# Both MLP products by Strassen's scheme in a one-core encoder layer

## The chip, the cores and the metric

The kernel runs on one core of a Trainium2 chip. The metric is the device time of one execution in microseconds; the kernel before has a median of 1634.68 us over three runs (1633.24 to 1635.64). A core has five engines that work side by side, each through its own instructions in a fixed order: TensorE (PE in the profile; PEld is its weight load) multiplies matrices into eight banks of a buffer called PSUM, VectorE (DVE), ScalarE (ACT) and GpSimd (POOL) work element by element, and SyncE (SP) here issues transfers between the on-chip buffer SBUF and DRAM. An instruction that waits holds up everything behind it on its engine.

## What is computed

One encoder layer on 1024 tokens of width 1024, all in float32. The first part (norm, pooling mixer, differential attention, gates, merge) is the same in both kernels. Behind it come the output projection and the MLP, of which the change speaks:

```python
x = x + merged @ w_out[l]
h2 = rmsnorm(x, g_ffn[l])
x = x + jnp.square(jax.nn.relu(h2 @ w_up[l])) @ w_down[l]   # w_up 1024 x 4096, w_down 4096 x 1024
```

## The kernel before

*Precision.* Every large product is done three times: `split` writes a float32 tile as a high part that TensorE multiplies exactly in its fast format (a cast on ScalarE, L114) and a low part, the rest (a subtraction on VectorE, or on GpSimd for weights, L115). `mm3` then issues three matmuls, high x high (L118), high x low (L119) and low x high (L120), that add up in one PSUM bank. A full matmul has 128 x 128 weights and moves 512 columns.

*Output projection.* `out_proj(ws, t, dh)` computes 128 tokens (tile t) by 512 columns (half dh) with 24 matmuls, and VectorE adds the result to x in SBUF (L815). The order of the calls is (th, dh) = (0,0), (0,1), (1,1), (1,0), with th the half of the tokens. As soon as both halves of a token tile are there, `late_norm` brings its second norm: ScalarE squares and sums (L254), `rsq` makes the factor with a small step on VectorE and a power on GpSimd (L236, L237), VectorE multiplies two halves by factor and gain (L258), TensorE transposes eight blocks (L263) and the result is split into h2T. These transposes stand between matmuls of later output projections and of the first up products.

*MLP.* Eight chunks of 512 of the 4096 inner columns. Per chunk eight up products (128 inner columns by 512 tokens, 24 matmuls each) are passed through relu (ScalarE, L863) and square (GpSimd, L864) and split into uT; then sixteen down products (128 tokens by 512 columns, 12 matmuls each) are added to y in SBUF (L886). Activations stay in SBUF. Weights come in loads of 512 KB on SP's queue; ScalarE and GpSimd split them.

*Order.* Tiles come from pools with a fixed number of buffers; a new tile waits until the readers of the one whose buffer it takes are through. The order of the instructions on each engine is set before the run by a scheduler that goes by its own simulated times; on the chip it is fixed.

## Time and profile before

| | |
|---|---|
| runs, us | 1633.24, 1634.68, 1635.64 |
| profiled execution, first to last instruction | 1631.6 us |
| what the runs have beyond that span | 1.6 to 4.0 us, 3.1 at the median |
| TensorE busy | 1613.1 us, 99% |
| VectorE, ScalarE, GpSimd busy | 46%, 40%, 36% |
| up products | from 916.8 us |
| last matmul | 1627.6 us |
| DRAM traffic | 98.0 MB read, 18.9 MB written |

The page shows no time of the profiled execution apart from its span, so the span stands for it. In the groups, a line reads: source line, engine, operation, written tile <- read tiles, shape, count, then busy time and the mean of one in ns; or, in the view of one tile, minimum/median/maximum of one in ns, the first and the last start in us, and the shapes. Timeline lines begin with start and duration in us. In the transfers the last number is the median time from issue to landing.

### The profile page before, as it was taken

How to read it: one execution, taken by the hardware profiler on the slowest of the kernel's cores; microseconds unless marked ns; L12 is line 12 of the kernel's file. 1: busy time of each engine (PE TensorE's matmuls, PEld its weight loads, DVE VectorE, ACT ScalarE, POOL GpSimd, SP SyncE). 2: the span in 40 equal slices, each digit the busy share in tenths (PEclk: the TensorE clock that was granted, in tenths of full speed). 3: DMA queues.
4: the chain of work that ended last, by engine and by line, in shares of the span. 5: the costliest groups of instructions: out<-in, count | busy, mean ns of one | idle time of the engine just before them, and what ended most of it. 6: DMA issues, size and time to landing. Idle time of an engine off the chain costs nothing.

```text
span 1631.6 us, 22018 instructions
## 1 busy us (share of the span) xinstructions
PE 1613.1 (99%) x8045; PEld 1395.0 (85%) x8045; DVE 758.0 (46%) x1962; ACT 655.0 (40%) x1600; POOL 580.5 (36%) x639
## 2 busy tenths in 40 slices
...
PEclk9999999999999999999999999999999999999999
...
GB/s 218 59 43 69 37 79 35 72 22 85 29 78 31 82 46 69 106 263 206 116 168 53 65 78 24 81 13 78 26 78 27 65 39 65 39 52 52 40 20 97
DMA packets 125575, 118.32 MB, mean 73 GB/s; under 512 B 5958, under 2 KB 99099, under 8 KB 125467
## 3 DMA queue, kind: packets, MB, share of 16 engines
...
q8 instruction: 63, 1.03, 0.3%
...
## 4 chain that ended last, share of the span: by engine, by line
PE 91%; DMA 3%; DVE 3%; ACT 1%; issue 1%; POOL 1%; SPq 0%; ACTq 0%; POOLq 0%; DVEq 0%
PE dn L119 7%; PE up L120 7%; PE dn L120 7%; PE dn L118 7%; PE up L118 7%; PE up L119 7%; PE z L120 5%; PE z L118 5%; PE z L119 5%; PE g L119 3%; PE g L118 3%; PE g L120 3%; PE sc L487 2%; PE sc L488 2%; PE ba L120 2%; PE op L120 2%
## 5 line engine op out<-in xcount | busy, mean ns | idle before, releaser
L886 DVE TENSOR_TENSOR y<-dn,y 128x512 f32<-128x512 f32 x129 | 88.7, 688 | 278.4 <-PE dn L120 278.4
L119 PE MATMUL dn<-wdn,uT 128*128 128x512 f32 (+1 forms) x516 | 199.9, 387 | 0.0
L120 PE MATMUL dn<-wdn,uT 128*128 128x512 f32 (+1 forms) x516 | 199.9, 387 | 0.0
L118 PE MATMUL dn<-wdn,uT 128*128 128x512 f32 (+1 forms) x516 | 199.9, 387 | 0.0
L118 PE MATMUL up<-h2T,wup 128*128 128x512 f32 x512 | 199.3, 389 | 0.0
L119 PE MATMUL up<-h2T,wup 128*128 128x512 f32 x512 | 199.3, 389 | 0.0
L120 PE MATMUL up<-h2T,wup 128*128 128x512 f32 x512 | 199.2, 389 | 0.0
L115 POOL TENSOR_TENSOR wup<-rup,wup 128x512 fp32r<-128x512 f32 x64 | 82.6, 1306 | 280.0 <-ACT wup L114 280.0
L115 DVE TENSOR_TENSOR uT<-rl,uT 128x512 fp32r<-128x512 f32 x64 | 59.3, 926 | 255.7 <-ACT uT L114 255.6
L118 PE MATMUL z<-wqkv,hT 128*128 128x384 f32 x512 | 174.9, 342 | 0.6 <-DVE qn L429 0.3
L120 PE MATMUL z<-wqkv,hT 128*128 128x384 f32 x512 | 174.8, 342 | 0.4 <-DVE hT L115 0.3
L119 PE MATMUL z<-wqkv,hT 128*128 128x384 f32 x512 | 174.1, 340 | 0.0
L114 ACT CAST wup<-rup 128x512 fp32r<-128x512 f32 x64 | 39.5, 623 | 273.5 <-PE dn L120 261.8
L237 POOL TENSOR_TENSOR ms<-ms,mhalf 128x4 f32<-128x4 f32 x64 | 66.6, 1041 | 158.8 <-DVE ms L236 139.8
L498 ACT ACTIVATE s<-s,nm 128x256 f32<-128x256 f32 (+7 forms) x128 | 99.8, 780 | 49.2 <-DVE nm L490 43.9
L118 PEld LDWEIGHTS dn<-wdn,uT 128*128 128x128 f32 x516 | 96.9, 188 | 19.8
L119 PEld LDWEIGHTS dn<-wdn,uT 128*128 128x128 f32 x516 | 96.9, 188 | 19.8
L120 PEld LDWEIGHTS dn<-wdn,uT 128*128 128x128 f32 x516 | 96.9, 188 | 19.7
L119 PEld LDWEIGHTS up<-h2T,wup 128*128 128x128 f32 x512 | 96.1, 188 | 19.9
L120 PEld LDWEIGHTS up<-h2T,wup 128*128 128x128 f32 x512 | 96.1, 188 | 19.9
L118 PEld LDWEIGHTS up<-h2T,wup 128*128 128x128 f32 x512 | 96.1, 188 | 19.9
L864 POOL TENSOR_TENSOR rl<-rl 128x512 f32<-128x512 f32 x64 | 70.1, 1095 | 107.8 <-ACT rl L863 99.2
...
## 6 DMA issues: line engine op xcount, KB each, us to landing
rup<-in_w_up_dram SPq DMA_DIRECT2D x32, 512.0 KB, 4.0
rdn<-in_w_down_dram SPq DMA_DIRECT2D x32, 512.0 KB, 4.0
...
frgate<-in_w_gate_dram SPq DMA_DIRECT2D x32, 256.0 KB, 2.8
g_dram<-go ACTq DMA_DIRECT2D x32, 256.0 KB, 4.1
ro<-in_w_out_dram SPq DMA_DIRECT2D x12, 512.0 KB, 4.6
y_dram<-oS ACTq DMA_DIRECT2D x32, 128.0 KB, 1.8
rb<-r_dram SPq DMA_DIRECT2D x8, 512.0 KB, 4.7
```

What stands on the lines that cost most here:

```text
L114: nc.scalar.copy(hi, src)
L115: (lo_eng or nc.vector).tensor_tensor(lo, src, f(hi), op=ALU.subtract)
L118: nc.tensor.matmul(ps, lhs_hi, rhs_hi, start=first, stop=False)
L119: nc.tensor.matmul(ps, lhs_hi, rhs_lo, start=False, stop=False)
L120: nc.tensor.matmul(ps, lhs_lo, rhs_hi, start=False, stop=last)
L237: nc.gpsimd.tensor_tensor(dst, dst, mhalf[:, :n], op=ALU.pow)
L487: nc.tensor.matmul(dst, Q[:, i, 0, :], rhs, start=True, stop=False)
L488: nc.tensor.matmul(dst, Q[:, i, 1, :], rhs, start=False, stop=True)
L498: nc.scalar.activation(s[i][:, 0:n], s[i][:, 0:n], AF.Exp, bias=last, scale=-1.0, accum_out=Z[:, i, t : t + 1])
L864: nc.gpsimd.tensor_tensor(rl, rl, rl, op=ALU.mult)
L886: nc.vector.tensor_tensor(ys, ps, ys, op=ALU.add)
```

## The change

Both MLP products go by Strassen's scheme in Winograd's form: both operands are cut into 2 x 2 blocks, and seven products of half-size blocks, made of sums and differences of blocks, replace eight. All that concerns the first part of the layer stays, and the first 4370 rows of TensorE's order are the same.

*Activations through DRAM.* The sum of the output projection is stored to a scratch tensor yd (L814). The pools of the first part are closed after the last output projection (`mix.close()`), and new ones opened in their place: 8 op tiles for split operands, 8 rw tiles for loaded data, smaller ones, 8 PSUM banks, and 14 tiles for the blocks of the normed activations. `norm_token` loads a token tile back (L882), norms it as before, and forms the right-hand blocks B11, B21, B22, T1 to T4: differences on VectorE, splits with the low parts on VectorE or GpSimd.

*Up.* `up_pair`, 16 times: two loads of 512 KB, the sums S1 to S4 of weight blocks on GpSimd, seven operand splits, seven products of 12 matmuls, relu and square, four differences of the results, and seven stores of 256 KB to the scratch tensors ud, which hold the left-hand blocks of the down product.

*Down.* Seven products in the order 1, 2, 6, 5, 7, 3, 4, each over the whole half depth in eight steps of 24 matmuls on four banks. A step loads 512 KB of ud and up to two 512 KB quarters of w_down, and splits both: casts on ScalarE, the low part of u on VectorE and of w on GpSimd. In the changed file the casts are L109, the low parts L110, the three matmuls L115 to L117. T1 and T2 of the weights are formed once and kept. Results are added to the residual or to each other on VectorE and stored.

Where instructions moved. The names are those of the program: op an output projection, hps or hb a bank of transposes, hm or hn a normed token tile, y a token tile, h2T and B11 the split activations. The first place is VectorE at the end of the output projection. Before:

```order
L815 TENSOR_TENSOR y_9712<-op_1_9886,y_9712 128x512
L815 TENSOR_TENSOR y_9990<-op_1_9992,y_9990 128x512
L115 TENSOR_TENSOR h2T_0_1_9853<-hps_0_9919,h2T_0_0_9852 128x2x128
L115 TENSOR_TENSOR h2T_0_1_9857<-hps_1_9929,h2T_0_0_9856 128x2x128
L236 TENSOR_SCALAR rs_9966<-ss_9965 128x1
L115 TENSOR_TENSOR h2T_0_1_9855<-hps_0_9919,h2T_0_0_9854 128x2x128
L115 TENSOR_TENSOR h2T_0_1_9859<-hps_1_9929,h2T_0_0_9858 128x2x128
L258 SCALAR_TENSOR_TENSOR hm_9964<-y_9712,rs_9966,gfb 128x512 x2
L815 TENSOR_TENSOR y_9740<-op_1_9938,y_9740 128x512
```

Now:

```order
L813 TENSOR_TENSOR y_9969<-op_0_10113,y_9969 128x512
L813 TENSOR_TENSOR y_9998<-op_0_10140,y_9998 128x512
L234 TENSOR_SCALAR nrs_10197<-nss_10196 128x1
L891 SCALAR_TENSOR_TENSOR hn_10195<-yt_10193,nrs_10197,gfb 128x512 x2
L110 TENSOR_TENSOR B11l<-hb_0_10202,B11h 128x4x128
L110 TENSOR_TENSOR B21l<-hb_1_10208,B21h 128x4x128
L234 TENSOR_SCALAR nrs_10233<-nss_10232 128x1
L891 SCALAR_TENSOR_TENSOR hn_10231<-yt_10229,nrs_10233,gfb 128x512 x2
```

Norms stood between the sums of the output projection; now the first norm (token 0) stands behind the last sum, and token 1's statistics behind token 0's splits. TensorE at the same place, from the last transposes on; before, an example of the transposes:

```order
L118 MATMUL op_1_9992<-wo_4_0_9786,mT_1_9400 128x512
L119 MATMUL op_1_9992<-wo_4_0_9786,mT_1_9400 128x512
L263 MATMUL hps_0_9867<-identf,hm_9860 128x128 x4
L263 MATMUL hps_1_9877<-identf,hm_9860 128x128 x4
L118 MATMUL op_1_9886<-wo_0_0_9770,mT_0_9077 128x512
L119 MATMUL op_1_9886<-wo_0_0_9770,mT_0_9077 128x512
```

Now, behind the last output projection and twelve rows of transposes of tokens 0 to 5:

```order
L895 MATMUL hb_0_10416<-identf,hn_10409 128x128 x4
L895 MATMUL hb_1_10422<-identf,hn_10409 128x128 x4
L895 MATMUL hb_0_10458<-identf,hn_10451 128x128 x4
L895 MATMUL hb_1_10464<-identf,hn_10451 128x128 x4
L115 MATMUL X_10551<-B11h,A_0_10553 128x512
L116 MATMUL X_10551<-B11l,A_0_10553 128x512
```

No output projection or up product is left between the transposes. The second place is GpSimd at the start of the up products (BT1l to BT3l low parts of T1 to T3, A and AS operand tiles of weights, s the sums S1 to S4, u the squares). Before, at the same place:

```order
L237 TENSOR_TENSOR rs_10020<-rs_10020,mhalf 128x1
L115 TENSOR_TENSOR wo_4_0_10146<-ro_4_10144,wo_4_0_10146 128x512
L115 TENSOR_TENSOR wo_4_1_10149<-ro_4_10144,wo_4_1_10149 128x512
L115 TENSOR_TENSOR wo_6_0_10154<-ro_6_10152,wo_6_0_10154 128x512
L115 TENSOR_TENSOR wo_6_1_10157<-ro_6_10152,wo_6_1_10157 128x512
L115 TENSOR_TENSOR wup_0_10352<-rup_10350,wup_0_10352 128x512
```

Now:

```order
L110 TENSOR_TENSOR BT1l<-t_7_10469,BT1h 128x4x128
L110 TENSOR_TENSOR BT2l<-t_7_10470,BT2h 128x4x128
L110 TENSOR_TENSOR BT3l<-t_7_10471,BT3h 128x4x128
L855 TENSOR_TENSOR s_0_10633<-wu_0_10547,wu_1_10549 128x512
L969 TENSOR_TENSOR u_0_10585<-u_0_10585 128x512
L858 TENSOR_TENSOR s_0_10634<-s_0_10633,wu_0_10547 128x512
L858 TENSOR_TENSOR s_0_10635<-wu_0_10547 128x512
L969 TENSOR_TENSOR u_1_10628<-u_1_10628 128x512
L858 TENSOR_TENSOR s_0_10636<-wu_1_10549,s_0_10634 128x512
L110 TENSOR_TENSOR AS_0_10657<-s_0_10633,AS_0_10657 128x512
```

The low part of S1 (AS_0) stands behind all low parts of T1 to T3. The third place is ScalarE in the down products; before, the weights of a chunk's down products were cast among the relus of its up products:

```order
L863 ACTIVATE rl_0_13625<-up_0_13600 128x512
L114 CAST wdn_0_0_13890<-rdn_0_13888 128x512
L114 CAST uT_0_13628<-rl_0_13625 128x512
L863 ACTIVATE rl_1_13656<-up_1_13631 128x512
L114 CAST wdn_0_1_13893<-rdn_0_13888 128x512
```

Now, at the start of product 6 (ur a loaded block of activations, T the kept T2 of the weights):

```order
L109 CAST u_7h<-ur_7_13707 128x1024
L109 CAST u_0h<-ur_0_13751 128x1024
L109 CAST w_0h<-T_0_13755 128x1024
L109 CAST u_1h<-ur_1_13789 128x1024
L109 CAST w_1h<-T_1_13793 128x1024
```

Both operands of each step are now cast in turn, one step after another. The diff, cut to its core (the removed MLP, which stands in the kernel above, down to its head):

```diff
+N_OP, N_RW, N_SM, N_EV = 8, 8, 4, 9
...
-        ys = y[t][:, dh * 512 : (dh + 1) * 512]
-        nc.vector.tensor_tensor(ys, ps, ys, op=ALU.add)
-    h2T = {}
-    gfb = ut([P, D], F32, "gfb")
-    nc.scalar.dma_start(gfb, g_ffn[0].partition_broadcast(P))
+        cs = slice(dh * 512, (dh + 1) * 512)
+        nc.vector.tensor_tensor(y[t][:, cs], ps, y[t][:, cs], op=ALU.add)
+        nc.sync.dma_start(yd[t * P : (t + 1) * P, cs], y[t][:, cs])
...
-    late = []
-    def late_norm():
-        if late:
-            t = late.pop(0)
-            if t % 4 == 0:
-                h2T.update(alloc_T(htile if t else ut, "h2T", t // 4))
-            hm = ut([P, D], F32, f"hm{t}")
-            norm_transpose(y[t], gfb, t, h2T, hm, fp, [(pb, "b")])
...
+    mix.close()
+    def pool_of(name, bufs, space=None):
+        kw = {} if space is None else {"space": space}
+        return ctx.enter_context(tc.tile_pool(name=name, bufs=bufs, reuse_waits="tile", **kw))
+    pw, pr, pe = pool_of("pw", N_OP), pool_of("pr", N_RW), pool_of("pe", 1)
+    bk = pool_of("bk", 8, PSUM)
...
+    hp = hs.enter_context(tc.tile_pool(name="hp", bufs=14, reuse_waits="tile"))
...
+    gfb = rw_tile([P, D], "gfb")
+    nc.sync.dma_start(gfb, g_ffn[0].partition_broadcast(P))
...
+    def b_split(q, c0, src, eng):
+        hi, lo = b_tile(q)
+        split(hi[:, :, c0 : c0 + P], lo[:, :, c0 : c0 + P], src, eng)
...
+    def norm_token(t):
+        th, c0 = t // 4, (t % 4) * P
+        yt = rw_tile([P, D], f"yt{t}")
+        nc.sync.dma_start(yt, yd[t * P : (t + 1) * P, :])
+        hn = rw_tile([P, D], f"hn{t}")
+        ss = pe.tile([P, 1], F32, tag="ss", name=f"nss{t}", bufs=2)
+        rs = pe.tile([P, 1], F32, tag="rs", name=f"nrs{t}", bufs=2)
+        nc.scalar.activation(hn, yt, AF.Square, accum_out=ss)
+        rsq(rs, ss, 1, 1.0 / D)
+        ps = []
+        for j in range(2):
+            js = slice(j * 512, (j + 1) * 512)
+            nc.vector.scalar_tensor_tensor(hn[:, js], yt[:, js], rs, gfb[:, js], op0=ALU.mult, op1=ALU.mult)
+            b = bank(f"hb{t}_{j}")
+            for i in range(4):
+                k = 4 * j + i
+                nc.tensor.transpose(b[:, i * P : (i + 1) * P], hn[:, k * P : (k + 1) * P], identf)
+            ps.append(b.rearrange("p (a b) -> p a b", a=4))
+        cs = slice(c0, c0 + P)
+        if th == 0:
+            for j, q in enumerate(("11", "21")):
+                if t == 0:
+                    Br[q] = [rw_tile([P, 2, 512], f"Br{q}_{i}") for i in range(2)]
+                b_split(q, c0, ps[j], dve)
+                for i in range(2):
+                    nc.scalar.copy(Br[q][i][:, :, cs], ps[j][:, 2 * i : 2 * i + 2, :])
+            return
+        t1, t2, t3, t4, b12 = (sm(f"{n}_{t}") for n in ("t1", "t2", "t3", "t4", "b12"))
+        nc.scalar.copy(b12, ps[0])
+        for i in range(2):
+            sub(dve, t1[:, 2 * i : 2 * i + 2, :], ps[0][:, 2 * i : 2 * i + 2, :], Br["11"][i][:, :, cs])
+        sub(dve, t2, ps[1], t1)
+        b_split("T2", c0, t2, pool)
+        b_split("T1", c0, t1, pool)
+        sub(dve, t3, ps[1], b12)
+        b_split("T3", c0, t3, pool)
+        b_split("22", c0, ps[1], dve)
+        for i in range(2):
+            sub(dve, t4[:, 2 * i : 2 * i + 2, :], Br["21"][i][:, :, cs], t2[:, 2 * i : 2 * i + 2, :])
+        b_split("T4", c0, t4, dve)
...
+    SIDES = {
+        "1": ("11", "11"), "2": ("12", "21"), "3": ("S4", "22"), "4": ("22", "T4"),
+        "5": ("S1", "T1"), "6": ("S2", "T2"), "7": ("S3", "T3"),
+    }
...
+    def u_product(ps, j, a):
+        hi, lo = Bq[SIDES[j][1]]
+        for k in range(4):
+            mm3(
+                ps, a[:, 0, k, :], a[:, 1, k, :], hi[:, k, :], lo[:, k, :],
+                j not in ADDS and k == 0, k == 3, j in ADDS,
+            )
+    def a_op(p, name, src, eng):
+        a = op([P, 2, 4, P], f"A{name}_{p}")
+        split(a[:, 0], a[:, 1], src, eng)
+        return a
...
+    def up_pair(p):
+        raws = []
+        for j in range(2):
+            r = rw_tile([P, 4, 2 * P], f"wu{p}_{j}")
+            nc.sync.dma_start(
+                r, w_up[j * 512 : (j + 1) * 512, p * 2 * P : (p + 1) * 2 * P].rearrange("(kk p) c -> p kk c", p=P)
+            )
+            raws.append(r)
+        A = {f"{i + 1}{j + 1}": raws[j][:, :, i * P : (i + 1) * P] for i in range(2) for j in range(2)}
+        X, Y = bank(f"X{p}"), bank(f"Y{p}")
+        u_product(X, "1", a_op(p, "11", A["11"], dve))
+        x1 = ev(f"x1_{p}")
+        nc.scalar.copy(x1, X)
+        u_product(Y, "2", a_op(p, "12", A["12"], pool))
+        C = {}
+        def finish(q, ps, part):
+            r = ev(f"u{q}_{p}")
+            add(dve, r, ps, part)
+            nc.scalar.activation(r, r, AF.Relu)
+            pool.tensor_tensor(r, r, r, op=ALU.mult)
+            C[q] = r
+        def store(name, src):
+            nc.sync.dma_start(ud[name, p // 2][:, p % 2, :], src)
+        finish("11", Y, x1)
+        store("11", C["11"])
+        yield
+        S1, S2, S3, S4 = (sm(f"s{i}_{p}") for i in range(1, 5))
+        add(pool, S1, A["21"], A["22"])
+        sub(pool, S2, S1, A["11"])
+        u_product(X, "6", a_op(p, "S2", S2, dve))
+        U2 = ev(f"U2_{p}")
+        nc.scalar.copy(U2, X)
+        Z = bank(f"Z{p}")
+        u_product(Z, "5", a_op(p, "S1", S1, pool))
+        z5 = ev(f"z5_{p}")
+        nc.scalar.copy(z5, Z)
+        sub(pool, S3, A["11"], A["21"])
+        u_product(X, "7", a_op(p, "S3", S3, dve))
+        U3 = ev(f"U3_{p}")
+        nc.scalar.copy(U3, X)
+        finish("22", X, z5)
+        store("22", C["22"])
+        sub(pool, S4, A["12"], S2)
+        u_product(Z, "3", a_op(p, "S4", S4, pool))
+        finish("12", Z, U2)
+        s1 = ev(f"us1_{p}")
+        add(dve, s1, C["12"], C["22"])
+        store("S1", s1)
+        s2 = ev(f"us2_{p}")
+        sub(dve, s2, s1, C["11"])
+        store("S2", s2)
+        s3 = ev(f"us3_{p}")
+        sub(dve, s3, C["11"], C["12"])
+        store("S3", s3)
+        W = bank(f"W{p}")
+        u_product(W, "4", a_op(p, "22", A["22"], dve))
+        finish("21", W, U3)
+        store("12", C["21"])
+        s4 = ev(f"us4_{p}")
+        sub(dve, s4, C["21"], s2)
+        store("S4", s4)
...
+    def quarter(j, q, ab, dh):
+        r = rw_tile([P, 2, 512], f"wd{j}_{q}_{ab}{dh}")
+        nc.sync.dma_start(r, wd[ab, :, q, :, dh * 512 : (dh + 1) * 512])
+        return r
...
+        if j == "1":
+            b11, b12 = quarter(j, q, 0, 0), quarter(j, q, 0, 1)
+            T1s[q] = kept("T1", q)
+            sub(dve, T1s[q], b12, b11)
+            return b11
...
+        if j == "6":
+            b22 = quarter(j, q, 1, 1)
+            T2s[q] = kept("T2", q)
+            sub(dve, T2s[q], b22, T1s[q])
+            return T2s[q]
+        if j == "7":
+            b22, b12 = quarter(j, q, 1, 1), quarter(j, q, 0, 1)
+            sub(dve, b22, b22, b12)
+            return b22
+        b21 = quarter(j, q, 1, 0)
+        sub(dve, b21, b21, T2s[q])
+        return b21
...
+    def operands(j, q):
+        ur = rw_tile([P, 2, 512], f"ur{j}_{q}")
+        nc.sync.dma_start(ur, ud[SIDES[j][0], q])
+        out_ = []
+        for n, src, eng in (("u", ur, dve), ("w", second(j, q), pool)):
+            hi, lo = (op([P, 2, 512], f"{n}{j}_{q}{x}") for x in "hl")
+            split(hi, lo, src, eng)
+            out_ += [hi, lo]
+        return out_
+    def d_step(banks, j, q, ops, ts):
+        uh, ul, wh, wl = ops
+        for i in range(2):
+            for t in ts:
+                c = slice(t * P, (t + 1) * P)
+                mm3(
+                    banks[t], uh[:, i, c], ul[:, i, c], wh[:, i, :], wl[:, i, :],
+                    j not in ADDS and q == 0 and i == 0, q == NQ - 1 and i == 1, j in ADDS,
+                )
...
+    def with_residual(banks, name, th, dh):
+        got = []
+        for t in range(4):
+            k = keep(f"{name}{t}")
+            add(dve, k, banks[t], residual(name, 4 * th + t, dh))
+            got.append(k)
+        return got
+    def finish_out(banks, parts, th, dh):
+        for t in range(4):
+            add(dve, parts[t], banks[t], parts[t])
+            r0 = (4 * th + t) * P
+            nc.sync.dma_start(out[r0 : r0 + P, dh * 512 : (dh + 1) * 512], parts[t])
...
+    d_product(DX, "1")
+    x1 = with_residual(DX, "x1y", 0, 0)
+    DY = four("DY")
+    d_product(DY, "2")
+    finish_out(DY, x1, 0, 0)
+    d_product(DX, "6")
+    U2 = with_residual(DX, "U2y", 0, 1)
+    DZ = four("DZ")
+    d_product(DZ, "5")
+    z5 = with_residual(DZ, "z5y", 1, 1)
+    d_product(DX, "7")
+    U3 = with_residual(DX, "U3y", 1, 0)
+    finish_out(DX, z5, 1, 1)
+    d_product(DZ, "3")
+    finish_out(DZ, U2, 0, 1)
+    DV = four("DV")
+    d_product(DV, "4", True)
+    finish_out(DV, U3, 1, 0)
...
-    NC = w_up.shape[1] // 512
-    for c in range(NC):
...
```

145 lines of the change are left out of this document (84 added, 61 removed).

## The prediction

> **What bounds the kernel now.** I read the page first (busy time, the 40 slices, the chain), then the MLP's instructions by tile and by line, then the stretches in which VectorE and GpSimd meet, and last the transfers.
>
> ```profile
> span 1631.6 us, 22018 instructions
> PE 1613.1 (99%) x8045; PEld 1395.0 (85%) x8045; DVE 758.0 (46%) x1962; ACT 655.0 (40%) x1600; POOL 580.5 (36%) x639
> ...
> PEclk9999999999999999999999999999999999999999
> ...
> PE 91%; DMA 3%; DVE 3%; ACT 1%; issue 1%; POOL 1%; SPq 0%; ACTq 0%; POOLq 0%; DVEq 0%
> ```
>
> TensorE is busy 99% of the span at full clock and carries 91% of the chain; the other engines are under half busy. So fewer matmuls are worth their full issue time, as long as the other engines keep the operands coming. The pace of a matmul is read from the evictions of the down products, each of which follows 12 matmuls:
>
> ```profile
> 1086.49 0.69 DVE L886 TENSOR_TENSOR y<-dn,y 128x512 f32<-128x512 f32 x1 [2.03 <-PE dn L120]
> ...
> 1105.53 0.69 DVE L886 TENSOR_TENSOR y<-dn,y 128x512 f32<-128x512 f32 x1 [2.03 <-PE dn L120]
> ```
>
> These are the first and the last of eight, with seven intervals between: 19.04 / 7 = 2.72 us for 12 matmuls, 0.2267 us each. (A matmul's own 389 ns overlaps its neighbours.)
>
> ```profile
> L118 PE MATMUL up<-h2T,wup x512: 389/389/474, 916.8 to 1583.4; 128*128 128x512 f32 x171
> L120 PE MATMUL dn<-wdn,uT 128*128 128x512 f32 x508 | 197.6, 389 | 0.0
> L120 PE MATMUL dn<-wdn,uT 128*128 128x256 f32 x8 | 2.3, 282 | 0.0
> L263 PE MATMUL hps<-identf,hm x64: 270/272/273, 872.8 to 947.4; 128*128 128x128 f32 x64
> 899.55 1.03 PE L263 MATMUL hps<-identf,hm 128*128 128x128 f32 x8
> 1627.60 0.28 PE L120 MATMUL dn<-wdn,uT 128*128 128x256 f32 x1
> 1627.91 0.42 DVE L886 TENSOR_TENSOR y<-dn,y 128x256 f32<-128x256 f32 x1 [1.01 <-PE dn L120]
> ```
>
> Each line stands for one of mm3's three matmuls, so the MLP has 3 x 512 + 3 x 508 = 3060 matmuls of 512 columns and 24 of 256 columns, the latter 0.12 us apart. From the first transpose at 872.8 to 1627.6 TensorE never waits, and the 64 transposes of the second norm lie inside this dense stretch.
>
> **The change part by part.**
>
> *Fewer matmuls.* Before: 3060 x 0.2267 + 24 x 0.12 = 696.6 us. After: 7 products x 16 pairs x 12 = 1344 for up and 7 x 8 steps x 24 = 1344 for down, 2688 x 0.2267 = 609.4 us. Term: -87.2.
>
> *The norm leaves the dense stretch.* In the order of the changed kernel all 16 groups of transposes stand behind the last output projection and ahead of the first X product. Eight transposes took 1.03 us, so 64 x 0.129 = 8.3 us leave the dense stretch. Term: -8.3. In exchange TensorE now waits for the norm, which nothing covers.
>
> ```profile
> L254 ACT ACTIVATE hm<-y x8: 1061/1064/1073, 865.8 to 939.9; 128x1024 f32<-128x1024 f32 x8
> 894.91 0.14 DVE L236 TENSOR_SCALAR rs<-ss 128x1 f32<-128x1 f32 x1
> 895.20 0.55 POOL L237 TENSOR_TENSOR rs<-rs,mhalf 128x1 f32<-128x1 f32 x1 [8.58 <-DVE rs L236]
> L258 DVE SCALAR_TENSOR_TENSOR hm<-y,rs,gfb x16: 743/752/1787, 868.5 to 944.5; 128x512 f32<-128x512 f32 x16
> ryT<-y_dram SPq DMA_DIRECT2D x8, 512.0 KB, 3.7
> L184 SPq DMA_DIRECT2D ryT<-y_dram x8: 319/320/320, 691.8 to 739.4; - x8
> rdn<-in_w_down_dram SPq DMA_DIRECT2D x32, 512.0 KB, 4.0
> y<-in_x_dram SPq DMA_DIRECT2D x8, 512.0 KB, 5.8
> ```
>
> *The gap.* Of the eight rw buffers gfb and the four Br tiles hold five; a token needs two (yt, hn). So the load of a token waits until an earlier token's transposes are through, and two tokens pass per round. A round is issue 0.32, load 3.7 to 4.0, Square 1.06 and its accumulator about 0.2, the two small steps 0.14 + 0.55, two multiplications 1.5, transposes 1.03: 8.5 to 8.8, with some five hand-overs of 0.1 to 0.15 us (895.05 to 895.20 is one) about 9.1. The first two tokens run one after the other, since VectorE's order has token 0's splits ahead of token 1's statistics: by the same durations they end 14 us after the last output matmul (gfb's load starts only some 2 us before that matmul, and yt0 stands behind it on SP's queue). Then rounds end at 23, 32 and, with the four differences and five splits of tokens 4 to 7 in the way, 43. The first X product starts near 44.
>
> *The ramp.* GpSimd's order puts twelve low parts of T1, T2, T3 and two of A12 ahead of S1 of pair 0. At 1.29 us each (row below), partly run during the rounds, S1's low part is ready about 65 us after the last output matmul if VectorE is never in the way, about 69 if its two-input subtractions alternate with GpSimd. By then TensorE has done 14.5 us of the products 1 and 2 of two pairs. So the loss is 69 - 14.5 = 54 us. Bounds: 44 if S1 comes in time, 70 if the loads take 5.8 as those of x did (four rounds x 1.8 = 7 more) and the ramp takes as much again. Term: +54, nearest to the rows of 3.7 and 4.0, since these loads read a scratch tensor in rows of the same length.
>
> *The clock after the gap.* No stretch behind the start has an idle TensorE, so only the start shows a cold one:
>
> ```profile
> 13.09 0.53 PE L118 MATMUL z<-wqkv,hT 128*128 128x384 f32 x1
> 13.41 0.53 PE L119 MATMUL z<-wqkv,hT 128*128 128x384 f32 x1
> ...
> 17.06 0.33 PE L118 MATMUL z<-wqkv,hT 128*128 128x384 f32 x1
> 17.23 0.33 PE L119 MATMUL z<-wqkv,hT 128*128 128x384 f32 x1
> ```
>
> 0.32 us from matmul to matmul, and 0.17 four us later. Bounds 0 (clock kept) and 4 (two cold stretches of 4 us, gap and ramp); term +2, one such stretch at half pace. The Trainium skill (TensorE: Matmul & The Clock Gate, Part 1) says that an idle window of about 3.4 us halves the clock and about 3.4 us of work restore it; by that the term would be 1.7 for each such idle stretch. The start agrees; that the clock also falls in mid-kernel no row here shows.
>
> *Up, in the steady state.* A pair is 7 x 2.72 = 19.04 us of TensorE.
>
> ```profile
> L115 POOL TENSOR_TENSOR wup<-rup,wup x64: 1282/1292/1747, 909.5 to 1540.6; 128x512 fp32r<-128x512 f32 x64
> L864 POOL TENSOR_TENSOR rl<-rl x64: 1035/1042/1492, 937.3 to 1584.9; 128x512 f32<-128x512 f32 x64
> L115 DVE TENSOR_TENSOR uT<-rl,uT x64: 682/694/1705, 941.6 to 1587.6; 128x512 fp32r<-128x512 f32 x64
> L114 ACT CAST wup<-rup x64: 612/625/642, 908.8 to 1539.4; 128x512 fp32r<-128x512 f32 x64
> L863 ACT ACTIVATE rl<-up x64: 585/599/617, 935.1 to 1584.2; 128x512 f32<-128x512 f32 x64
> ```
>
> GpSimd per pair: four sums S1 to S4 and three low parts at 1.29, four squares at 1.04: 13.2 us. VectorE: four low parts and four differences for the store with two SBUF inputs, 8 x 0.69 = 5.5, and four sums out of PSUM, 2.8. ScalarE: 7 x 0.62 + 8 x 0.60 = 9.1. Each fits in 19.04, and the order gives the operands a lead of 15 us or more. Two loads of 512 KB and seven stores of 256 KB, 2.8 MB in 19 us = 147 GB/s. Term 0, covered by the 19.04 us.
>
> *Down, in the steady state.* A step is 24 matmuls, 5.44 us, and needs four op tiles of eight: those of the step after next come free when this step ends. The chain from there: ScalarE casts u and w (1.1 each; its pass of 128x1024 took 1.06), GpSimd's low part of w 2.6 (two of 1.29): 4.8 us, 6.1 if a subtraction of VectorE (1.28) goes first. It is needed after four high-high matmuls of the step after, at 5.44 + 0.91 = 6.35. So 0.2 to 1.5 us to spare: term 0 for the steps. Its transfers: 1.05 MB in 5.44 us = 193 GB/s; products 1 and 7 load two quarters, 1.57 MB = 289 GB/s.
>
> ```profile
> core 0: us, PE busy (x) PEld busy (x) DVE busy (x) ACT busy (x) POOL busy (x), PEclk, DMA share, GB/s
> 715.00:725.00 10.00, 10.00 (x46) 8.29 (x45) 4.38 (x6) 4.15 (x7) 2.61 (x2) 1.00 0.90 317
> ```
>
> The kernel has moved 317 GB/s while TensorE stayed dense, so even these fit, with little room. Change-overs (up to down, where the last activations go to DRAM and come back before product 4 needs them, and six between products): bounds 0, if the loads run ahead as the order has them, and 15, if the first step waits for a store (2.0), a load (4.0), the casts (2.2) and the low part (2.6) and the others for 0.7 each; I take 6, as SP issues the first product's loads before the last stores.
>
> *The end.* The last sum is a full 512 columns instead of 256 (0.69 for 0.42) and the last store 256 KB instead of 128:
>
> ```profile
> out_dram<-y SPq DMA_DIRECT2D x15, 256.0 KB, 2.0
> out_dram<-y SPq DMA_DIRECT2D x2, 128.0 KB, 1.8
> ```
>
> Term +0.5.
>
> **Sum:** -87.2 - 8.3 + 54 + 2 + 6 + 0.5 = -33.0. The profiled span was 1631.6; the median of the runs is 1634.7, 3.1 above it. 1634.7 - 33 = 1602.
>
> **The rivals.**
>
> *B, slower: VectorE and GpSimd exclude each other in the up products.* What speaks for it:
>
> ```profile
> 736.81 2.52 POOL L115 TENSOR_TENSOR wbp<-rbp,wbp 128x512 fp32r<-128x512 f32 x2 [14.47 <-ACT wbp L114]
> 738.16 2.26 DVE L188 SCALAR_TENSOR_TENSOR ryT<-ryT,gs,rb 128x1024 f32<-128x1024 f32 x1 [5.31 <-DMA ryT<-y_dram]
> L188 DVE SCALAR_TENSOR_TENSOR ryT<-ryT,gs,rb x8: 1279/1284/2256, 695.8 to 742.9; 128x1024 f32<-128x1024 f32 x8
> ```
>
> A two-input operation of VectorE took 2.26 us beside GpSimd's split and 1.28 alone: it stood still until the split ended at 739.33. If the two never overlap, a pair needs 13.2 + 5.5 = 18.7 of its 19.04 us. Against it: 18.7 is still less than 19.04, and back to back GpSimd took 1.26. For it: any time in which both wait cannot be caught up. Were a pair 20.6 to 22 us, 16 x 1.6 to 3.0 = 25 to 47 us would go: 1627 to 1649. From 33 / 16 = 2.1 us per pair it decides. The Trainium skill (SBUF — State Buffer, Who interferes with whom) states it as a rule: a VectorE instruction with two SBUF inputs and a GpSimd instruction that reads SBUF hold one shared port in turn, whoever is second is blocked entirely. The pair of rows at 736.81 and 738.16 agrees.
>
> *C: the down steps are bound by the chain of casts or by the transfers.* For it: two steps of buffers, 0.2 us to spare in the worst order, 289 GB/s. Against it: ScalarE is 2.2 of 5.44 us busy, GpSimd 2.6. At 6.0 us on the 32 steps with a subtraction it costs 18 (1620), on all 56 it costs 31 (1633); from 33 / 56 = 0.6 us per step it is slower than before.
>
> *D: the gap is shorter.* If the two tokens of a round overlap, so that a round takes 7 us, and S1 is ready in time, TensorE loses 34 us in place of 54: 1582, and 1574 without change-overs and cold clock. Against it stands the single queue of the loads.
>
> *E: several orders that the scheduler fixed by its own times do not fit the chip's,* and engines wait on each other throughout: with 1.5 us on each of 16 pairs and 0.6 on each of 56 steps, 58 us, it comes to 1660. For it speaks only that no row shows the new order; against it that each engine alone has 6 us per pair to spare.
>
> **How the numbers follow.** My forecast 0.60 (gap 44 to 70, change-overs 0 to 15, clock 0 to 4: 1584 to 1629); B 0.14, of which 0.06 faster, 0.01 the same, 0.07 slower; C 0.11, of which 0.05, 0.01 and 0.05; D 0.07; E 0.08. Faster: 0.60 + 0.06 + 0.05 + 0.07 = 0.78; within 0.2% (3.3 us, about what the three runs differ by) 0.02; slower 0.07 + 0.05 + 0.08 = 0.20. The range from 1577 to 1650 leaves out E and half of D.
>
> **What would show it.** Right: the slices of TensorE show one hole of 50 to 60 us behind 924 us and are full elsewhere; transposes in four rounds of 9 us; pairs 19.04 us apart by the stores of u; down sums of one product 43.5 us behind the last. Wrong: idle time of TensorE put down to GpSimd's AS or w low parts in the steady state (B, C), steps of 6 us or more in products 1 and 7 (C by transfers), or a hole outside 44 to 70 us.

## The result, and the profile after

The changed kernel took 1634.73 us in the median of 12 runs (1631.18 to 1639.20), the kernel before 1633.84 us (1631.76 to 1635.64) beside it: a ratio of 1.0008 [0.9998, 1.0017]. That is no change. The prediction was 1602, so 32.7 us of the gain went elsewhere. The profiled run took 1636.88 us. From the page of the changed kernel: span, busy times, TensorE and its clock in 40 slices, and the shares of the chain that ended last.

```profile
span 1635.1 us, 22296 instructions
...
PE 1557.7 (95%) x7649; PEld 1334.0 (82%) x7649; DVE 966.0 (59%) x2089; ACT 766.2 (47%) x1712; POOL 736.6 (45%) x691
...
PE   7999999999999999999999748999999999899999
...
PEclk9999999999999999999999959999999999999999
...
PE 80%; DVE 8%; DMA 5%; POOL 3%; issue 2%; ACT 2%; SPq 0%; ACTq 0%; POOLq 0%; DVEq 0%
```

TensorE is busy for 55 us less (1613.1 before) and stands idle for 59 us more: it is busy 95% instead of 99%. There is one hole (slices of 7, 4 and 8) with the clock down beside it, and a thin place near 1420 us (the 8). What the slices don't show are waits shorter than a slice. The view of TensorE's waits lists them (engine, line and operand, the releaser: us in total, times, longest):

```profile
PE hb L895 <- DVE hn L891: 24.5, 8, 6.4
PE Z L115 <- DVE u L855: 12.5, 9, 1.4
...
PE X L115 <- ACT AS L109: 6.1, 1, 6.1
PE DX L117 <- DVE u_1l L110: 4.4, 1, 4.4
...
PE DX L116 <- POOL w_4l L110: 1.2, 1, 1.2
```

hb are the transposes of the norm in the gap, X with AS the start of product 6 at the ramp, both forecast. The second row was not: nine times, the product Z waits for a sum of VectorE.

**The gap.** Timeline of TensorE: the last output projection, two groups of transposes, the first X product, and the first product that needs S2.

```profile
929.05 0.39 PE L117 MATMUL op<-wo,mT 128*128 128x512 f32 x1
...
935.81 1.94 PE L895 MATMUL hb<-identf,hn 128*128 128x128 f32 x8 [6.37 <-DVE hn L891]
942.58 1.94 PE L895 MATMUL hb<-identf,hn 128*128 128x128 f32 x8 [4.83 <-DVE hn L891]
...
974.08 0.78 PE L115 MATMUL X<-B11h,A 128*128 128x512 f32 x1
...
993.69 0.79 PE L115 MATMUL X<-BT2h,AS 128*128 128x512 f32 x1 [6.08 <-ACT AS L109]
```

The last matmul's slot ends at 929.28, so X starts 44.8 us later, and the sums are there 64.4 us later. In between TensorE did 48 matmuls of the next pairs, 10.9 us of work, so 53.5 us were lost. The transposes of tokens 1, 3, 5 and 7 end about 15, 24, 32 and 45 us behind the last output matmul. The same stretch in windows (busy us of each engine, granted clock, DMA share, GB/s):

```profile
core 0: us, PE busy (x) PEld busy (x) DVE busy (x) ACT busy (x) POOL busy (x), PEclk, DMA share, GB/s
924.00:940.00 16.00, 7.38 (x33) 5.73 (x31) 4.33 (x7) 3.80 (x9) 0.56 (x1) 0.82 0.45 155
...
950.00:960.00 10.00, 4.30 (x18) 3.58 (x19) 7.11 (x14) 6.53 (x17) 1.10 (x2) 0.50 0.39 140
960.00:970.00 10.00, 3.70 (x16) 2.56 (x14) 9.65 (x18) 7.77 (x14) 7.46 (x7) 0.50 0.32 101
970.00:980.00 10.00, 6.98 (x26) 5.11 (x27) 8.35 (x12) 5.11 (x11) 6.10 (x5) 0.73 0.50 162
```

The clock falls to half in mid-kernel, and eight transposes take 1.94 us there.

**The up products.** Timeline of TensorE over two pairs in the steady state: X opens a pair, Z waits.

```profile
1102.27 0.40 PE L115 MATMUL X<-B11h,A 128*128 128x512 f32 x1
...
1109.40 0.47 PE L115 MATMUL Z<-BT1h,AS 128*128 128x512 f32 x1 [1.38 <-DVE u L855]
...
1144.56 0.40 PE L115 MATMUL X<-B11h,A 128*128 128x512 f32 x1
...
1151.69 0.47 PE L115 MATMUL Z<-BT1h,AS 128*128 128x512 f32 x1 [1.38 <-DVE u L855]
```

From 1102.27 to 1144.56 there are two pairs, 21.15 us each, where 19.04 was forecast. Two things make the difference. Twelve matmuls take 2.785 us here and not 2.72 (0.45 us per pair), and each Z loses 1.63 us with its restart. Z needs no operand then; it needs its PSUM bank. The bank it gets was W, which product 4 of an earlier pair filled about 28 us before, by 1123.4, and which nobody has read yet. The reader is the sum u21 (`finish("21", W, U3)`), and VectorE's queue shows where it stands:

```profile
1146.86 1.77 DVE L855 TENSOR_TENSOR us<-u,u 128x512 f32<-128x512 f32 x1 [2.41 <-POOL u L969]
1148.67 1.67 DVE L858 TENSOR_TENSOR us<-us,u 128x512 f32<-128x512 f32 x1
1150.26 0.68 DVE L858 TENSOR_TENSOR us<-u,u 128x512 f32<-128x512 f32 x1
1150.86 0.68 DVE L855 TENSOR_TENSOR u<-W,U 128x512 f32<-128x512 f32 x1
```

GpSimd's queue in the same moments:

```profile
1145.79 1.04 POOL L969 TENSOR_TENSOR u<-u 128x512 f32<-128x512 f32 x1
1146.79 1.30 POOL L110 TENSOR_TENSOR AS<-s,AS 128x512 fp32r<-128x512 f32 x1
1148.16 1.62 POOL L858 TENSOR_TENSOR s<-wu,s 128x512 f32<-128x512 f32 x1
```

VectorE waits for GpSimd's square of u12, then makes us1, us2 and us3, and only then reads the bank. us1 and us2 take 1.77 and 1.67 us instead of the 0.68 of us3, because GpSimd works on SBUF beside them: each ends 0.5 to 0.6 us behind GpSimd's row beside it (the split that ends at 1148.09, the sum s that ends at 1149.78).

**The down products.** All steps take 5.44 us, as forecast, but five: steps 0, 1 and 4 of product 1 lose 1.08, 1.75 and 4.09 us, steps 0 and 1 of product 6 lose 1.21 and 6.35. Timeline of ScalarE in step 4 of product 1, and then of VectorE and TensorE at the start of product 6:

```profile
1334.28 1.06 ACT L109 CAST u_4h<-ur 128x1024 fp32r<-128x1024 f32 x1 [6.84 <-DMA ur<-ud]
...
1411.59 2.47 DVE L855 TENSOR_TENSOR x1y<-DY,x1y 128x512 f32<-128x512 f32 x4
1413.98 1.21 DVE L858 TENSOR_TENSOR T<-wd,T 128x1024 f32<-128x1024 f32 x1
1415.12 3.35 DVE L110 TENSOR_TENSOR u_1l<-ur,u_1h 128x1024 fp32r<-128x1024 f32 x1
...
1418.53 0.50 PE L117 MATMUL DX<-w_1h,u_1l 128*128 128x512 f32 x1 [4.45 <-DVE u_1l L110]
...
1419.53 0.63 PE L116 MATMUL DX<-w_1l,u_1h 128*128 128x512 f32 x1
```

The windows in which the load for step 4 was under way, and behind it (columns as above):

```profile
1328.00:1335.00 7.00, 7.00 (x33) 5.79 (x32) 7.00 (x5) 0.72 (x1) 4.68 (x2) 1.00 0.99 324
1340.00:1360.00 20.00, 19.74 (x80) 16.17 (x81) 17.57 (x10) 7.36 (x8) 9.57 (x5) 0.91 1.04 401
```

In step 4 of product 1 the load of u came late. It was issued at 1328.47, when a subtraction T1 on VectorE had freed its buffer, and took 5.8 us (4.3 in the median) with the DMA engines full (share 0.99, 324 GB/s; 401 behind it). In product 6 the low part of u stood on VectorE behind a subtraction T2 that had itself waited 1.6 us for its quarter of w_down, four sums and one more T2, and then took 3.35 us instead of 1.21. After the wait of 4.45 us the matmuls run 0.43 us apart, so TensorE pays again in clock.

### The profile page after: what moved, and what is told of

It reads as the page before. It is cut to its first block, busy times and chain, and to the rows that moved or that the text cites. A ratio compares the mean times of both kernels' runs of the same rounds, so it can differ in the third digit from the quotient of the medians.

```text
span 1635.1 us, 22296 instructions
## 1 busy us (share of the span) xinstructions
PE 1557.7 (95%) x7649; PEld 1334.0 (82%) x7649; DVE 966.0 (59%) x2089; ACT 766.2 (47%) x1712; POOL 736.6 (45%) x691
## 4 chain that ended last, share of the span: by engine, by line
PE 80%; DVE 8%; DMA 5%; POOL 3%; issue 2%; ACT 2%; SPq 0%; ACTq 0%; POOLq 0%; DVEq 0%
PE z L117 5%; PE z L115 5%; PE z L116 5%; PE g L115 3%; PE g L116 3%; PE g L117 3%; PE DX L117 3%; PE DX L116 3%; PE DX L115 2%; PE X L115 2%; PE sc L485 2%; PE sc L486 2%; PE X L116 2%; PE X L117 2%; PE Z L115 2%
## 5 line engine op out<-in xcount | busy, mean ns | idle before, releaser
L115 PE MATMUL z<-wqkv,hT 128*128 128x384 f32 x512 | 175.0, 342 | 0.3 <-DVE qn L427 0.2
L117 PE MATMUL z<-wqkv,hT 128*128 128x384 f32 x512 | 174.6, 341 | 0.5 <-DVE hT L110 0.5
L116 PE MATMUL g<-hT,fwgate 128*128 128x512 f32 x256 | 101.0, 394 | 0.0
L117 PE MATMUL g<-hT,fwgate 128*128 128x512 f32 x256 | 101.0, 394 | 0.0
L115 PE MATMUL g<-hT,fwgate 128*128 128x512 f32 x256 | 100.9, 395 | 0.0
L115 PEld LDWEIGHTS z<-wqkv,hT 128*128 128x128 f32 x512 | 96.9, 189 | 4.2 <-DVE qn L427 0.8
L117 PEld LDWEIGHTS z<-wqkv,hT 128*128 128x128 f32 x512 | 96.9, 189 | 3.2 <-DVE hT L110 1.3
L116 PEld LDWEIGHTS z<-wqkv,hT 128*128 128x128 f32 x512 | 97.0, 189 | 3.0
L969 POOL TENSOR_TENSOR u<-u 128x512 f32<-128x512 f32 x64 | 72.9, 1139 | 43.1 <-ACT u L968 43.1
L488 DVE CUSTOM_DVE_ANT_0 s<-sc,dist 128x512 f32<-128x512 f32 (+3 forms) x128 | 74.7, 586 | 22.3 <-PE sc L486 20.7
L110 POOL TENSOR_TENSOR wqkv<-rqkv,wqkv 128x384 fp32r<-128x384 f32 x60 | 63.3, 1073 | 20.0 <-ACT wqkv L109 18.2
L968 ACT ACTIVATE u<-u 128x512 f32<-128x512 f32 x64 | 40.4, 632 | 65.4 <-DVE u L855 65.0
L110 POOL TENSOR_TENSOR fwgate<-frgate,fwgate 128x512 fp32r<-128x512 f32 x32 | 45.0, 1408 | 53.3 <-ACT fwgate L109 53.2
L485 PE MATMUL sc<-K,Q 128*128 128x512 f32 (+2 forms) x192 | 67.4, 356 | 0.1
L486 PE MATMUL sc<-K,Q 128*128 128x512 f32 (+2 forms) x192 | 66.6, 354 | 0.0
L109 ACT CAST AS<-s 128x512 fp32r<-128x512 f32 x64 | 39.5, 620 | 55.6 <-PE X L117 19.9
L110 DVE TENSOR_TENSOR AS<-s,AS 128x512 fp32r<-128x512 f32 x32 | 37.1, 1160 | 45.4 <-ACT AS L109 45.1
```

What stands on the lines that cost most here:

```text
L109: nc.scalar.copy(hi, src)
L110: (lo_eng or nc.vector).tensor_tensor(lo, src, f(hi), op=ALU.subtract)
L115: nc.tensor.matmul(ps, lhs_hi, rhs_hi, start=first, stop=False, **kw)
L116: nc.tensor.matmul(ps, lhs_hi, rhs_lo, start=False, stop=False, **kw)
L117: nc.tensor.matmul(ps, lhs_lo, rhs_hi, start=False, stop=last, **kw)
L485: nc.tensor.matmul(dst, Q[:, i, 0, :], rhs, start=True, stop=False)
```

## The experiments

Each ratio is to the kernel before on the same chip, and what a run gained over the changed kernel is the difference of its ratio to 1.0008, times 1635 us.

### Is it the order of VectorE's queue that stops Z?

Product 4 and its sum out of bank W go ahead of us1, us2 and us3.

```diff
         finish("12", Z, U2)
 
+        W = bank(f"W{p}")
+        u_product(W, "4", a_op(p, "22", A["22"], dve))
+        finish("21", W, U3)
         s1 = ev(f"us1_{p}")
...
-        W = bank(f"W{p}")
-        u_product(W, "4", a_op(p, "22", A["22"], dve))
-        finish("21", W, U3)
         store("12", C["21"])
```

> Edit: in every pair of up products the product 4 (bank W) and its sum stand ahead of the three differences us1 to us3 in the program, so VectorE empties bank W first. Theory O (order): in the changed kernel the first matmul of product 5 waits 1.54 us in nine pairs for VectorE's sum out of the bank W that it takes over, and this sum stands behind us1 and us2, which wait for GpSimd's square and then take 1.77 and 1.67 us beside GpSimd. With the sum ahead of them the wait goes: pairs 19.5 us apart in place of 21.15, 12 to 15 us less than the changed kernel's 1634.7, so about 1621. Rival P (port): the pair is held by VectorE and GpSimd excluding each other, whatever the order; then another wait takes its place, pairs stay near 21 us and the time within 4 us of 1634.7.

Measured: 1619.50 us, ratio 0.9907 [0.9893, 0.9922], 16.5 us less than the changed kernel. The pairs come 19.60 us apart, no wait of Z for u is left, and us1 still has a median of 1.53 us (duration in ns: least, median, most):

```profile
L855 DVE TENSOR_TENSOR us<-u,u x16: 693/1525/2871, 1016.4 to 1310.9; 128x512 f32<-128x512 f32 x16
```

So the wait goes while the sums stay slow. But the edit moved more than VectorE's queue: the scheduler also gave TensorE another order. Product 4 now ends beside product 3 of its own pair, so that its bank is read 0.6 us later (27.7 before), and product 5, which opens Z, stands behind product 6.

### Or is it GpSimd beside VectorE?

All work of GpSimd on tensors in up goes to the other engines: the sums S1 to S4 and the low parts to VectorE, the squares to ScalarE. VectorE's order of us1 to u21 stays.

```diff
-            pool.tensor_tensor(r, r, r, op=ALU.mult)
+            nc.scalar.activation(r, r, AF.Square)
...
-        add(pool, S1, A["21"], A["22"])
+        add(dve, S1, A["21"], A["22"])
...
-        u_product(Z, "5", a_op(p, "S1", S1, pool))
+        u_product(Z, "5", a_op(p, "S1", S1, dve))
...
-        u_product(Z, "3", a_op(p, "S4", S4, pool))
+        u_product(Z, "3", a_op(p, "S4", S4, dve))
```

> Edit: in the up products the sums S1 to S4 and all low parts go to VectorE and the squares to ScalarE, so that GpSimd has nothing to do there; the order of VectorE's us1, us2, us3 ahead of the sum from bank W is as in the changed kernel. Theory P (port): us1 and us2 take 1.77 and 1.67 us in place of 0.69 because GpSimd holds the port; without GpSimd the sum from bank W comes 2 us earlier, the wait of 1.54 us goes and pairs come 19.5 to 19.6 us apart: 1619 to 1623. Theory O (order alone): what counts is the wait for the square of the products ahead of us1; it is then ScalarE's, 0.6 us in place of 1.04, and the pair shortens too. If the wait goes, us1's own duration (0.69 or still 1.7) tells which. Rival: VectorE, with 13 us of work in a pair, is late by its own queue: pairs stay above 20.5 us and the time above 1630.

Measured: 1617.41 us, ratio 0.9892 [0.9877, 0.9906], 19 us less, a little more than expected. The pairs again come 19.60 us apart. The tile of the sums for the store, first in the changed kernel:

```profile
L855 DVE TENSOR_TENSOR us<-u,u x16: 678/1768/1777, 1018.8 to 1334.8; 128x512 f32<-128x512 f32 x16
L858 DVE TENSOR_TENSOR us<-us,u x16: 693/1667/1670, 1020.6 to 1335.5; 128x512 f32<-128x512 f32 x16
```

and with GpSimd idle:

```profile
L855 DVE TENSOR_TENSOR us<-u,u x16: 677/692/692, 1011.0 to 1310.5; 128x512 f32<-128x512 f32 x16
L858 DVE TENSOR_TENSOR us<-us,u x16: 691/693/2841, 1011.7 to 1311.2; 128x512 f32<-128x512 f32 x16
```

So the sums are slow because of GpSimd, and in the changed kernel their slowness reaches TensorE because they stand ahead of the only reader of a bank. Which of the two is enough to cure it, these runs don't separate: here too the scheduler gave TensorE the new order (bank W is read 4.2 us after it is filled). In both runs Z comes 8.4 us behind the start of X, where its old place was 5.6. In the changed kernel the sum out of W ended 7.0 us behind X, so the new place of Z may have sufficed by itself. With the new order of VectorE the sum ends at 1.0 us and with GpSimd idle at 4.7, early enough for the old place too; that either would do without TensorE's new order is argued from these times, not run.

That the slowness comes from a shared port is what the Trainium skill (SBUF — State Buffer, Who interferes with whom) says of an instruction with two SBUF inputs; 1.77 us beside GpSimd and 0.69 without it agree. This edit moves the squares too, which releases us1 earlier; these two effects weren't tried apart in up either.

### Why twelve matmuls take 2.785 us

The operand that moves through TensorE in up is a block of the normed activations (B11 and the others; A holds the weights). These blocks start at another offset in SBUF than the split tiles of before did. An unused tile of 480 columns (1920 bytes), behind the pools of A and of the loads and ahead of the blocks, moves the blocks.

```diff
     bk = pool_of("bk", 8, PSUM)
+    pool_of("px", 1).tile([P, 480], F32, name="pad")
```

> Edit: an unused tile of 1920 bytes per partition ahead of the blocks of the normed activations, which moves their addresses; nothing else changes. In the changed kernel twelve up matmuls take 2.785 us from start to start, those of the down products and of all of the kernel before 2.72. Theory A (address): the place of the moving operand sets it; with the addresses at the same offset as the split tiles of before (1440 bytes past a multiple of 4096 in place of 3616) twelve take 2.72 and the time falls by 4 to 6 us (part of the gain is taken up by the wait for VectorE in nine pairs). Rival: the pace has another cause (the order of products, the waits); 2.785 and the time stay.

Measured: 1629.76 us, ratio 0.9975 [0.9962, 0.9988], 5.4 us less; twelve matmuls take 2.72 us. The first matmuls of products 3 and 4, twelve matmuls apart, in the changed kernel:

```profile
1117.84 0.39 PE L115 MATMUL Z<-B22h,AS 128*128 128x512 f32 x1
...
1120.63 0.40 PE L115 MATMUL W<-BT4h,A 128*128 128x512 f32 x1
```

and with the pad:

```profile
1133.86 0.39 PE L115 MATMUL Z<-B22h,AS 128*128 128x512 f32 x1
...
1136.58 0.39 PE L115 MATMUL W<-BT4h,A 128*128 128x512 f32 x1
```

A pad of 32 columns (128 bytes) tells which part of the address counts.

```diff
+    pool_of("px", 1).tile([P, 32], F32, name="pad")
```

> Edit: the unused tile ahead of the blocks is 128 bytes per partition in place of 1920; the rest is the changed kernel. The blocks then lie 160 bytes past a multiple of 512 (32 in the changed kernel, where twelve up matmuls take 2.785 us; 416 in the run with 1920 bytes, where they take 2.72). If the offset modulo 256 counts (160 in both), twelve take 2.72 us; if only 416 modulo 512 is good, 2.785.

Measured, one run: 1631.01 us; twelve matmuls take 2.72 us again. By the sizes of the tiles (the trace shows no addresses) the blocks start 32 bytes behind a multiple of 256 in the changed kernel, and 160 behind one in both padded kernels, as the split tiles of before did. So the pace of this matmul depends on where its moving operand starts, and 128 bytes decide. Other offsets weren't tried.

### The norm ahead of the gap

The norm moves into the stage of the output projection: as soon as a token's y is complete, its square sum and product are made, and hn goes to a scratch tensor `hd`. In the gap only hn is loaded and transposed.

```diff
+    hd = dram.tile([S, D], F32, name="hd")
...
+        nc.scalar.activation(hm, y[t], AF.Square, accum_out=ss)
+        rsq(rs, ss, 1, 1.0 / D)
...
+        nc.scalar.dma_start(hd[t * P : (t + 1) * P, :], hm)
...
-        yt = rw_tile([P, D], f"yt{t}")
-        nc.sync.dma_start(yt, yd[t * P : (t + 1) * P, :])
         hn = rw_tile([P, D], f"hn{t}")
...
+        nc.sync.dma_start(hn, hd[t * P : (t + 1) * P, :])
```

> Edit: statistics and scaling of the second norm are done between the output projections, as in the kernel before, from the tile in SBUF, and the normed tile goes to a scratch tensor; behind the last output projection it is only loaded, transposed and split. Theory G: the stretch between the last output matmul and the first X product (44.8 us in the changed kernel) is a chain of load, square, scale and transposes with two tokens in flight. Without its middle the tokens are bound by ScalarE's and VectorE's passes, some 2.7 us each for tokens 0 to 3 and 4.5 to 5 for 4 to 7: about 33 us to the first X product, 10 to 14 us less than 1634.7, so about 1623. Rival: the loads and the splits set it; then the stretch stays above 41 us and the time within 4 us.

Measured: 1609.16 us, ratio 0.9849 [0.9832, 0.9866], 26 us less, about twice what was expected. Timeline of TensorE, the last output projection and the first X product:

```profile
925.48 0.39 PE L117 MATMUL op<-wo,mT 128*128 128x512 f32 x1
945.30 0.50 PE L115 MATMUL X<-B11h,A 128*128 128x512 f32 x1 [1.45 <-ACT A L109]
```

and its waits:

```profile
PE X L115 <- ACT AS L109: 13.6, 1, 13.6
...
PE hb L909 <- DMA hn<-hd: 7.2, 4, 3.8
```

X starts 19.6 us behind the output projection and not 44.8. The wait moves on to the ramp: 13.6 us for the operands of product 6 (6.1 before), so gap and ramp together lose 34.1 us instead of 53.5. Of the 26 us, some 5 are not the norm's: its small tiles are gone from the pool ahead of the blocks, which moves the blocks, and twelve matmuls take 2.72 us here.

### Does the cold clock matter in the gap?

Transposes that nobody reads fill the gap, 45 ahead of the first token and 16 behind each but the last.

```diff
+    fb = bank("fill")
+    for _ in range(45):
+        nc.tensor.transpose(fb[:, 0:P], identf, identf)
     for t in range(NT):
         norm_token(t)
+        c0 = (t % 4) * P
+        src = Br["11"][0][:, 0, c0 : c0 + P] if t < 4 else f(Bq["T2"][0][:, 0, c0 : c0 + P])
+        for _ in range(16 if t < NT - 1 else 0):
+            nc.tensor.transpose(fb[:, 0:P], src, identf)
```

> Edit: transposes whose result nobody reads fill TensorE's idle time behind the last output matmul: 45 ahead of token 0, 16 behind each of the next seven tokens, on operands that stay where they are anyway. Theory C (clock): in the changed kernel the granted clock is 0.50 from 940 to 970 us, so that eight transposes take 1.94 us in place of about 1.0 and the first 62 up matmuls lose 5 us. Kept busy, the clock stays near 1.00, the eight transposes take about 1.0, and 4 to 7 us go: 1628 to 1631. Rival: the idle time between two tokens still lets the clock fall, or the filling delays the tokens: clock 0.5 or the same stretch of 44 to 45 us, and the time within 3 us of 1634.7 or above it.

Measured: 1635.17 us, ratio 1.0004 [0.9995, 1.0013], the same as the changed kernel, as the rival had it. The windows of the gap:

```profile
940.00:950.00 10.00, 7.66 (x46) 6.71 (x44) 4.49 (x9) 5.45 (x14) 1.20 (x3) 0.74 0.22 82
950.00:960.00 10.00, 7.63 (x41) 7.06 (x42) 5.47 (x9) 5.48 (x15) 1.00 (x2) 0.66 0.32 107
```

The clock was kept only in part, and the filler delayed the tokens: X started 49 us behind the output projection. What a full clock would be worth in the gap stays open.

### The change-overs of the down products

First theory: product 6 starts late because the quarters of w_down have too few buffers. They get four of their own.

```diff
-        r = rw_tile([P, 2, 512], f"wd{j}_{q}_{ab}{dh}")
+        r = pd.tile([P, 2, 512], F32, tag="wq", name=f"wd{j}_{q}_{ab}{dh}", bufs=4)
```

> Edit: in the down products the quarters of w_down get four buffers of their own beside the eight that the activations are then alone in. Theory L (loads): the 14.5 us that TensorE loses in products 1 and 6 (steps 0, 1 and 4 of 1, steps 0 and 1 of 6) come from VectorE's subtractions T1 and T2, which stand ahead of the low parts of the current step and wait for quarters that find no free buffer. With buffers of their own the loads run ahead, and 6 to 12 us of the 14.5 go: 1623 to 1629. Rival: the transfers themselves are too slow there (401 GB/s in one stretch); then the same steps stay long and the time within 3 us of 1634.7.

Measured: 1647.48 us, ratio 1.0084 [1.0069, 1.0099], 12 us more. TensorE's waits:

```profile
PE X L115 <- ACT U L983: 6.5, 1, 6.5
PE DX L117 <- DVE u_1l L110: 5.4, 1, 5.4
...
PE DX L115 <- ACT w_0h L109: 2.4, 1, 2.4
```

For product 6 the theory falls: its step 1 still waits 5.4 us for u's low part. And the new buffers lie where tiles of up lie until its end, so the first load of w_down, which in the changed kernel had run ahead into the shared buffers at 1230.4 us, is issued only at 1311.3, with up near its end. The first and third row stand at that change-over. Steps 1 and 4 of product 1 lose 0.1 us and nothing here; since up is over by then, that does not show what held them.

Second theory: GpSimd's low parts of w slow VectorE down there. They go to VectorE itself.

```diff
-        for n, src, eng in (("u", ur, dve), ("w", second(j, q), pool)):
+        for n, src, eng in (("u", ur, dve), ("w", second(j, q), dve)):
```

> Edit: in the down products the low part of w moves from GpSimd to VectorE, so that GpSimd is idle there; the rest is the changed kernel. Theory Q (queue and port): the 14.5 us that TensorE loses in products 1 and 6 come from VectorE's queue: subtractions T1 and T2 and the sums of the product before stand ahead of the low part that TensorE needs, and beside GpSimd's split (2.4 us) an operation of 1.22 us takes 2.3 to 3.4. With GpSimd idle each takes 1.22 and the low part of w 1.2 in place of 2.4: the long steps of products 1 and 6 lose 2 us together in place of 12 to 14, 7 to 12 us less than 1634.7, so 1623 to 1628. Rival: VectorE, now with up to 3.7 us of work in a step of 5.44, is late in every step; then the steps are over 5.6 us throughout and the time is above 1640.

Measured: 1631.43 us, ratio 0.9976 [0.9967, 0.9986], 5 us less, above the range that the theory gave. Product 6 loses 3.7 us in place of 7.6 and product 1 about 2.8 in place of 6.9, but in products 7, 3 and 4 VectorE is now late at times, and the down stage loses 9.8 us in place of 14.5. So GpSimd is part of the cause at these two places, and elsewhere its help is worth more than it costs.

### The causes taken away together

Three edits at once: the early norm, product 4 ahead of us1, and VectorE for w's low part.

> Edit: the earlier norm, the sum from bank W ahead of the differences, and the low part of w on VectorE in the down products, all three at once. If the parts are independent: 1609 with the earlier norm, whose pace is already 2.72 us per twelve matmuls; nine pairs at 19.04 in place of 20.80 take off 16; the down steps 7 to 12: 1581 to 1587, faster than both kernels. If one part only moves the wait to another place, above 1595.

Measured: 1591.48 us, ratio 0.9731 [0.9712, 0.9750], some 4 us above the expected range: step 1 of product 1 took 11.75 us, since w's low part on VectorE came 3.5 us late there and the matmuls behind it ran at half pace. With VectorE for w in product 6 alone:

```diff
+        for n, src, eng in (("u", ur, dve), ("w", second(j, q), dve if j in "6" else pool)):
```

> Edit: as the run with three edits at once (1591.5), but VectorE makes the low part of w in product 6 alone; in the other products GpSimd does, as in the changed kernel. There VectorE was late in steps of products 1, 7, 3 and 4 (11.7 us for step 1 of product 1, 4.1 us over in steps of 7, 3 and 4). Theory Q: these go and product 6 keeps its short steps; product 1 loses 4 to 7 us as in the run with the sum from bank W first: 1584 to 1588. Rival: product 1 is held by the stores and loads of its activations whatever the engine: within 2 us of 1591.5.

Measured: 1587.31 us, ratio 0.9706 [0.9690, 0.9722]. All steps of products 7, 3 and 4 take 5.44 us again but for one of 5.49. Last, the squares of up on ScalarE as well:

```diff
-            pool.tensor_tensor(r, r, r, op=ALU.mult)
+            nc.scalar.activation(r, r, AF.Square)
```

> Edit: as the run before it in this list, and the squares on ScalarE in place of GpSimd. If the port still costs at the start of the up products (GpSimd has the low parts of T1 to T3 and S1 to S4 there) and at the change to the down products, 1 to 4 us less than that run; if ScalarE's longer queue delays the casts of the operands, as much more.

Measured: 1581.93 us, ratio 0.9671 [0.9653, 0.9689], 5.4 us less than the kernel ahead of it (a little more than expected), and 3.3% faster than the kernel before. By the two profiles the down products lose 4.4 us less (product 1 now loses nothing), gap and ramp 2 us less. What is left of TensorE's larger waits in the MLP:

```profile
PE X L115 <- ACT AS L109: 11.7, 1, 11.7
...
PE hb L909 <- DMA hn<-hd: 7.3, 4, 4.6
...
PE DX L116 <- DVE w_0l L110: 2.4, 1, 2.4
```

So Strassen's scheme does pay in this kernel, once the gap is shortened and the bank, the pace and the change-overs are mended.

## Why the prediction was wrong

The terms against the two profiles (spans 1631.6 and 1635.1):

| term | predicted, us | measured, us |
|---|---|---|
| fewer matmuls | -87.2 | -80.2 |
| transposes out of the dense stretch | -8.3 | -6.3 |
| gap and ramp | +54 | +53.5 |
| clock behind it | +2 | +2.7 |
| up, steady state | 0 | +14.6 |
| down, steps and change-overs | +6 | +14.5 |
| the end | +0.5 | 0 |
| ahead of the change | none | +5.2 |
| sum | -33.0 | +4.0 (spans: +3.5) |

*Gap and ramp: the gap right, the sum with some luck.* X came 44.8 us behind the output projection (44 said), by the rounds that were forecast (14, 23, 32 and 43 us said); making the norm early took 25 us from the gap. S1's low part was ready at 69.3 us (69 said), but product 6 comes first and needs S2, which was ready at 64.4. And the work in between was 10.9 us and not 14.5: products 1 and 2 of two pairs are 48 matmuls. The two slips, 4.6 and 3.6 us, nearly cancel. The clock's fall was a bound without a row; now the rows show it, 0.50 from 940 to 970. The Trainium skill (TensorE: Matmul & The Clock Gate, Part 1) has the rule that an idle window halves the clock. The trace agrees with it in mid-kernel. How long a wait must be the rows leave open: the clock stayed full behind the 2.2 us of TensorE at 736.8 in the kernel before (an idle stretch that the prediction passed over), and it fell in product 1 of the changed kernel behind waits of 1.25 and 0.58 us. At the start, where the prediction read four us, half pace lasted from 8.26 to about 16 us.

*"Up, in the steady state", term 0: wrong, and the step that failed.* The argument there was that each engine has time to spare per pair and that the operands have a lead of 15 us. The first is true (VectorE is busy 11.4 us and GpSimd 13.4 of 21.15), and no product waits for an operand in these pairs. Both miss the wait: it is not for an operand but for a PSUM bank, whose last reader stands behind slower work in VectorE's in-order queue. Rival B named the right pair of engines (VectorE and GpSimd in each other's way), but reasoned with total time, 18.7 of 19.04 us, and got 0.14. That its range of 1627 to 1649 holds the result is luck: the wait cost 14.6 us and not B's 25 to 47, in nine of the 16 pairs, and of the 2.1 us per pair there 0.45 are the pace. The durations acted through a queue: us1 and us2, lengthened by 2 us together, put off the sum by more than the bank could wait. The wait is gone in the two runs that put the sum first or leave GpSimd idle, both with TensorE's order changed as well.

*"Fewer matmuls": the count was right, the price was not.* 0.2267 us for each was read from products whose moving operand starts 160 bytes behind a multiple of 256; in up it starts 32 behind one, and twelve take 2.785 us. 16 pairs x 7 x 0.065 us is 7 us. The pad got back 5.4; in the nine pairs with the wait, the wait took up a part.

*"Change-overs, I take 6": too small.* The bound was 15, and 14.5 was measured; that the two are close is luck, since five of the six changes between products cost nothing. The reason to take less than half of the bound, loads issued ahead of the last stores, held for the first loads alone: the load of u for step 4 of product 1 was issued when VectorE had freed a buffer, and landed late. In product 6 buffers of their own didn't shorten the wait, and a shorter queue of VectorE did (7.6 to 3.7 us); waits for quarters of w_down stand in that queue too, and what they cost was not tried apart. Rival C, that the steps are bound, is wrong: of 56 steps 51 take 5.44 us.

*Transposes: 2 us too much.* Eight in the dense stretch cost 0.79 us by their spacing; 1.03 was the duration of the group with its tail.

*Ahead of the change: open.* In the profile of the changed kernel the output projection starts at 842.2 us, before at 837.0, with the same instructions ahead of it. Of these 5.2 us 4.6 arise between 736 and 747 us: the wait for wbp there is 3.9 us and was 2.2, and behind it TensorE runs at half pace until 746.6, which it did not before. Over the profiles of the changed kernel and its variants that wait lies between 2.6 and 5.7 us, and the start between 838.7 and 843.0. What makes the wait longer was not settled. A part is chance of the two profiled executions: that of the changed kernel is 2.2 us above its median, and the medians differ by 0.9 us where the spans differ by 3.5.

Two misjudgements of 14.6 and 8.5 us, two prices together 9 us off, and 5.2 us from elsewhere make the 37 us between -33.0 and +4.0. The forecast of "faster" rested on 33 us into which every wait that was set at 0 could only eat: a term of 0 for a wait is never wrong downwards.
